# A decoder layer on one core: where the second MLP product's tiles are folded, and when its operands are made

## The chip, the cores and the metric

The kernel runs on one core of a Trainium2 chip. The metric is the device time of one execution in microseconds (us); of several executions the median is given. The engines named below are PE (TensorE, matrix products, with its weight loads as PEld), DVE (VectorE), ACT (ScalarE), POOL (GpSimd) and SP (SyncE, which issues loads). Each works through its own queue in order; an instruction that waits holds up all that stand behind it on its engine.

## The reference, cut to what matters

One layer with 512 tokens and a model width of 1024, in float32:

```python
x = x + mix                                                   # two token mixers, gated
h2 = rmsnorm(x, ln2[i])
x = x + jnp.square(jax.nn.relu(h2 @ w_mlp1[i])) @ w_mlp2[i]   # 1024 -> 4096 -> 1024
h3 = rmsnorm(x, ln3[i])
x = x + jax.nn.sigmoid(h3 @ w_pg[i]) * (p[i] @ w_pp[i])
return rmsnorm(x, ln_f)
```

The change lies in the product with `w_mlp2` and in what follows it: the residual sum, the squares for the norm with `ln3`, and the transposes that the product with `w_pg` needs.

## The kernel before

**Products in three terms.** Each float32 operand is split into a high half that PE takes as it is and a low half, the rest. A product is then three: high by high, low by high, high by low. ACT makes the high half (`hi`, line 319 for weights, 461 for activations), DVE the low one (line 297 for both, shown as `lo` for weights and `ur` for activations).

**The second MLP product in pieces.** The 4096 hidden columns are four chunks. Chunk 0 is done plainly, in two products (`m2_plain`, one for each half of the output columns, four weight units each). Chunks 1 to 3 are done with seven products each in place of eight (Strassen's method, in Winograd's form): A11, S1, S2, S4, A12, S3 and A22 name the weights, and B11, T1, T2, B22, B21, T3 and T4 the hidden operands that go with them. These 21 products stand in the list `MLP2`, which fixes their order; chunks add up in the same PSUM banks, so a bank is complete when its product of chunk 3 is done. A product has two weight units of 128 x 1024, here called half products, with 12 matmuls each, in groups of three. The order of the 21 is A11.1, S1.1, S2.1, A11.2, S1.2, S4.1, S2.2, A11.3, S1.3, S4.2, S2.3, A12.1, S4.3, A12.2, S3.1, S3.2, S3.3, A12.3, A22.1, A22.2, A22.3, with the chunk behind the dot.

**Weights ahead of use.** `weight` calls `fetch`, which at the start of a half product issues the low half for the one two places on (DVE), the high half for the one three on (ACT), the sum that makes S2 or the last S4 four on (DVE, lines 263 and 266), and the loads five on; the first load of S1 and S3 is issued sooner still (SP, line 242), with a second load on POOL's queue that adds to it in place (line 250; line 314 for S4). There are 5 buffers for high halves, 4 for low ones and 8 for raw weights, so a low half cannot be written before PE has left the half product four places back.

**Side work.** Whatever else is to be done is put between the matmuls by `step`, called after each group of three in the 21 products and each eight matmuls in the plain ones. It runs the first entry of the list `later`, and it takes a generator in `side` one stage further each time that `pace` columns (4608 here, nine matmuls of 512) have gone by:

```python
def step(columns=None):
    if later:
        later.pop(0)()
    since[0] += columns or together[0] * pace[0]
```

`hid_operands` is such a generator: for each of the 21 products in their order it makes the sum (two DVE instructions, line 1418 or 609; T products only), then the two high halves (ACT), then the two low ones (DVE). Before the change it is put into `side` between the two plain products.

**The fold.** A token tile of the residual is `x2[m, t, n]`: column half m, token half t, tile n. `onto` (line 1455, DVE) adds a bank or a tile times the norm's factor to it. In Winograd's form the seven products make shared sums: p (A11), u = p + a (bank a is S2's) and w = u + c (bank c is S1's). Tile (0,0) gets p and bank b (A12), (0,1) gets w and bank d (S4), (1,1) gets w and bank x (S3), and (1,0) gets u and bank x after A22 has been added to it. `final` folds the last bank of a tile, squares the tile for the norm (ACT, line 1481), transposes it (PE, line 1486, four transposes, called a turn here) and splits the transposed tile. In the kernel before, p is copied and folded behind A11 of chunk 3; all of u and w is made and folded behind S2 of chunk 3 (`a_done`, `c_done`, `w_done`, lines 1508, 1512 and 1455), which this document calls the joint; and each `final` stands directly behind the last product of its bank.

**Inputs of the end.** The rows of p and the factor of the last norm are loaded on POOL's queue (lines 1548 and 1552) ahead of the 21 products, and p is split as an entry of `later`.

## Time and profile before

| what | value |
|---|---|
| time, median of 3 runs (lowest to highest) | 957.88 us (956.86 to 957.93) |
| profiled execution: its own time | 956.95 us |
| profiled execution: span | 955.1 us |
| instructions | 15091 |
| mean granted clock of PE | 0.995 |
| second MLP product in the span | 726 to 891 us |
| moved by DMA | 150.34 MB, mean 157 GB/s |

The page's second part cuts the span into 40 slices of 23.9 us; the second MLP product is in the 31st to the 38th:

```profile
PE   9999999999999999999999999999999999989997
DVE  7698879866789589878856797677766698997454
PEclk9999999999999999999999999999999999999998
DMA  9474482973818456456562437556557556796202
```

Each digit is a busy share in tenths, 9 being 90% or more. A busy PE is a PE that has a matmul in flight; the granted clock says how fast it may go. A wait is put down to what released it last.

### The profile page before, as it was taken

How to read it: one execution, taken by the hardware profiler on the slowest of the kernel's cores; microseconds unless marked ns; L12 is line 12 of the kernel's file. 1: busy time of each engine (PE TensorE's matmuls, PEld its weight loads, DVE VectorE, ACT ScalarE, POOL GpSimd, SP SyncE). 2: the span in 40 equal slices, each digit the busy share in tenths (PEclk: the TensorE clock that was granted, in tenths of full speed). 3: DMA queues.
4: the chain of work that ended last, by engine and by line, in shares of the span. 5: the costliest groups of instructions: out<-in, count | busy, mean ns of one | idle time of the engine just before them, and what ended most of it. 6: DMA issues, size and time to landing. Idle time of an engine off the chain costs nothing.

```text
span 955.1 us, 15091 instructions
## 1 busy us (share of the span) xinstructions
PE 944.7 (99%) x5892; PEld 851.2 (89%) x5892; DVE 726.7 (76%) x1029; ACT 541.0 (57%) x880; POOL 103.2 (11%) x143
## 2 busy tenths in 40 slices
PE   9999999999999999999999999999999999989997
PEld 8789998899988888999988899999998888868886
DVE  7698879866789589878856797677766698997454
ACT  7357546445675579675723447555655356556543
POOL 0150010120100013021020000011000110010000
PEclk9999999999999999999999999999999999999998
DMA  9474482973818456456562437556557556796202
GB/s 349 141 229 118 128 199 68 293 231 95 199 45 232 157 152 176 123 133 199 157 219 88 128 71 197 135 133 155 156 150 186 149 117 147 217 268 199 67 0 89
DMA packets 46022, 150.34 MB, mean 157 GB/s; under 512 B 6723, under 2 KB 7311, under 8 KB 45952
## 3 DMA queue, kind: packets, MB, share of 16 engines
q1 hardware_dynamic: 29664, 100.61, 30.7%
q0 software_dynamic: 12608, 44.26, 23.5%
q10 hardware_dynamic: 3680, 4.51, 1.3%
q8 instruction: 46, 0.75, 0.3%
q14 instruction: 24, 0.20, 0.1%
HBM read 143.03 MB, written 8.17 MB: 158 GB/s over the span
## 4 chain that ended last, share of the span: by engine, by line
PE 96%; DVE 3%; issue 1%; ACT 0%; POOL 0%; POOLq 0%; DVEq 0%
PE mmt L333 76%; PE smt L333 9%; PE mmt L581 2%; PE smt L1015 1%; DVE lo L297 1%; PE smt L955 1%; PE smt L878 1%; PE smt L553 0%; DVE u L1455 0%; DVE ur L297 0%; PE smt L848 0%; PE smt L972 0%; PE smt L971 0%; PE smt L961 0%; PE smt L847 0%
## 5 line engine op out<-in xcount | busy, mean ns | idle before, releaser
L333 PE MATMUL mmt<-ur,hi 128*128 128x256 f32 (+1 forms) x2320 | 476.0, 302 | 0.0
L333 PEld LDWEIGHTS mmt<-ur,hi 128*128 128x128 f32 x2320 | 373.4, 188 | 16.7
L333 PE MATMUL mmt<-ur,lo 128*128 128x256 f32 (+1 forms) x1160 | 351.2, 303 | 0.0
L297 DVE TENSOR_TENSOR lo<-w,hi 128x1024 fp32r<-128x1024 f32 x248 | 301.3, 1218 | 58.5 <-PE mmt L333 37.4
L319 ACT ACTIVATE hi<-w 128x1024 fp32r<-128x1024 f32 x248 | 259.1, 1054 | 91.5 <-PE mmt L333 21.7
L333 PE MATMUL mmt<-hi,ur 128*128 128x512 f32 (+3 forms) x832 | 240.9, 373 | 0.0
L333 PEld LDWEIGHTS mmt<-ur,lo 128*128 128x128 f32 x1160 | 218.6, 188 | 8.1
L333 PEld LDWEIGHTS mmt<-hi,ur 128*128 128x128 f32 x832 | 150.5, 188 | 25.8
L333 PE MATMUL mmt<-lo,ur 128*128 128x512 f32 (+3 forms) x416 | 154.9, 372 | 0.0
L461 ACT ACTIVATE ur<-u 128x512 fp32r<-128x512 f32 x111 | 66.3, 625 | 88.7 <-DVE u L1279 30.9
L333 PEld LDWEIGHTS mmt<-lo,ur 128*128 128x128 f32 x416 | 78.2, 188 | 13.9 <-DVE lo L297 0.3
L297 DVE TENSOR_TENSOR ur<-u,ur 128x512 fp32r<-128x512 f32 x110 | 72.4, 684 | 12.2 <-ACT ur L461 9.9
L333 PE MATMUL smt<-hi,ur 128*128 128x512 f32 x256 | 80.4, 396 | 0.0
L454 DVE TENSOR_TENSOR u<-u,mmt 128x512 f32<-128x512 f32 (+1 forms) x88 | 54.1, 646 | 26.8 <-PE mmt L333 26.5
L401 ACT ACTIVATE u<-mmt 128x512 f32<-128x512 f32 x72 | 43.0, 598 | 52.7 <-PE mmt L333 52.5
L250 POOL DMA_DIRECT2D w<-in_wts_dram x42 | 40.0, 1005 | 232.5 <-DVE lo L297 72.9
L333 PEld LDWEIGHTS smt<-hi,ur 128*128 128x128 f32 x256 | 48.4, 191 | 9.8
L333 PE MATMUL smt<-lo,ur 128*128 128x512 f32 x128 | 50.6, 395 | 2.0 <-DVE lo L297 2.0
L276 POOL DMA_DIRECT2D w<-in_wts_dram x18 | 16.1, 897 | 316.4 <-DVE w L273 153.5
L333 PEld LDWEIGHTS smt<-lo,ur 128*128 128x128 f32 x128 | 24.4, 191 | 7.6 <-DVE lo L297 2.4
L1389 ACT ACTIVATE u<-u 128x512 f32<-128x512 f32 x24 | 15.0, 628 | 26.7 <-DVE u L1385 26.7
L1250 ACT ACTIVATE u<-u 128x256 f32<-128x256 f32 x32 | 11.4, 409 | 20.8 <-DVE u L454 20.7
(235 smaller groups left out, 838.9 us busy)
## 6 DMA issues: line engine op xcount, KB each, us to landing
w<-in_wts_dram SPq DMA_DIRECT2D x180, 512.0 KB, 4.6
w<-in_wts_dram POOLq DMA_DIRECT2D x64, 512.0 KB, 7.3
u<-in_xT_dram SPq DMA_DIRECT2D x8, 256.0 KB, 5.3
u<-in_ws_dram SPq DMA_DIRECT2D x8, 256.0 KB, 5.4
v_dram<-u ACTq DMA_DIRECT2D x8, 256.0 KB, 6.3
u<-v_dram POOLq DMA_DIRECT2D x8, 256.0 KB, 6.4
y_dram<-u ACTq DMA_DIRECT2D x8, 256.0 KB, 2.0
u<-y_dram POOLq DMA_DIRECT2D x8, 256.0 KB, 6.3
```

The costliest lines, as they stand in the source:

```text
L250: GP.dma_start(w, wts[UNIT[b]], accum_op=OP.add)
L276: GP.dma_start(w, wts[UNIT[f"{q}.A21"]], accum_op=OP.add)
L297: V.tensor_tensor(lo, x, hi.bitcast(F32), op=OP.subtract)
L319: S.activation(hi[:, s], w[:, s], AF.Copy, scale=1.0 if c is None else c)
L333: TE.matmul(o, lhsT=l, rhs=r, start=a, stop=b, skip_group_check=shared)
L401: S.activation(sums[c], bank[b], AF.Copy, scale=-scale if c[0] else scale)
L454: V.tensor_tensor(out, s, ps, op=OP.subtract if m else OP.add)
L461: S.activation(hi, x, AF.Copy)
L581: TE.matmul(q0ps[i], lhsT=(hi, hi, lo)[j][:, c], rhs=(xh, xl, xh)[j], start=not k and not j, stop=k == KC - 1 and j == 2)
L878: TE.matmul(pss[b // 2][:, a * 256 + lo:a * 256 + 256], lhsT=q0[h][:, b * P:(b + 1) * P], rhs=k0[h][:, (b - 1) * P + lo:(b + 1) * P], star ...
L1250: S.activation(outs[n], s[:, halves(n)], AF.Sigmoid)
L1389: S.activation(s, s, AF.Square)
```

## The change

The number and the kind of the sums and folds stay; their places and the tiles that hold them change.

- Behind A11 of chunk 3, p is only copied (ACT), into a tile s of its own. Behind S2 of chunk 3, u and w are only made, each in tiles of its own.
- w is folded onto (0,1) behind A12 of chunk 2 and onto (1,1) behind S3 of chunk 2. s and u are folded onto (0,0) and (1,0) behind A12 of chunk 3.
- `final` of (0,1) stands behind S3 of chunk 1 rather than behind S4 of chunk 3. The others stay behind the product that they stood behind.
- `hid_operands` is put into `side` as soon as the plain operands are split, two weight units before the end of the first plain product.
- The loads of p and of the last norm's factor go behind S3 of chunk 3, and p's split behind A22 of chunk 2.

```diff
@@ m2_plain
             if len(hs) < 8:
                 hid_splits(2)
+                if len(hs) == 8:
+                    side.append(hid_operands())
...
+    def last_inputs():
+        for k in range(2):
+            t = u32()
+            GP.dma_start(t, pT[k * P:(k + 1) * P, :])
+            pt.append(t)
+        for g in range(2):
+            t = u32()
+            GP.dma_start(t, lnf[:, g * 512:(g + 1) * 512].to_broadcast([P, 512]))
+            lnb.append(t)
...
         def p_done(n):
-            u.append(u32())
-            S.activation(u[n], bank["p"][n], AF.Copy)
-            onto(0, 0, n, bank["p"][n])
+            s.append(u32())
+            S.activation(s[n], bank["p"][n], AF.Copy)
 
         def a_done(n):
-            V.tensor_tensor(u[n], u[n], bank["a"][n], op=OP.add)
-            onto(1, 0, n, u[n])
+            u.append(u32())
+            V.tensor_tensor(u[n], s[n], bank["a"][n], op=OP.add)
 
         def c_done(n):
-            V.tensor_tensor(u[n], u[n], bank["c"][n], op=OP.add)
-
-        def w_done(n):
-            for m in range(2):
-                onto(m, 1, n, u[n])
+            w.append(u32())
+            V.tensor_tensor(w[n], u[n], bank["c"][n], op=OP.add)
+
+        def onto_w(m):
+            return lambda n: onto(m, 1, n, w[n])
+
+        def onto_u(n):
+            onto(1, 0, n, u[n])
+
+        def onto_s(n):
+            onto(0, 0, n, s[n])
+
+        last = SEVEN[-1]
+        after = {("A11", last): [p_done], ("S2", last): [a_done, c_done], ("A12", 2): [onto_w(0)], ("S3", 1): [(0, 1, "d", smt)],
+                 ("S3", 2): [onto_w(1)], ("S3", last): [(1, 1, "x", mmt)], ("A12", last): [onto_s, (0, 0, "b", smt), onto_u],
+                 ("A22", last): [(1, 0, "x", smt)]}
...
-            for f in {"A11": (p_done,), "S2": (a_done, c_done, w_done)}.get(op, ()):
-                later.extend(lambda f=f, n=n: f(n) for n in range(2))
-            if op in ("S4", "S3", "A12", "A22"):
-                (m, t), turns = {"S4": ((0, 1), smt), "S3": ((1, 1), mmt), "A12": ((0, 0), smt), "A22": ((1, 0), smt)}[op]
+            for f in after.get((op, c), ()):
                 for n in range(2):
-                    final(m, t, n, bank[b][n], turns)
+                    if callable(f):
+                        later.append(lambda f=f, n=n: f(n))
+                    else:
+                        final(*f[:2], n, bank[f[2]][n], f[3])
+            if (op, c) == ("S3", last):
+                last_inputs()
+            elif (op, c) == ("A22", 2):
+                later.append(lambda: pt.__setitem__(slice(0, 2), [split(t) for t in pt]))
...
     m2_plain(0)
-    side.append(hid_operands())
     m2_plain(1)
-    for k in range(2):
-        t = u32()
-        GP.dma_start(t, pT[k * P:(k + 1) * P, :])
-        pt.append(t)
-    for g in range(2):
-        t = u32()
-        GP.dma_start(t, lnf[:, g * 512:(g + 1) * 512].to_broadcast([P, 512]))
-        lnb.append(t)
-    later.append(lambda: pt.__setitem__(slice(0, 2), [split(t) for t in pt]))
     m2_seven()
```

## The prediction, as it was made before the changed kernel ran

> **What bounds the kernel now.** I read the busy shares first, then the stretches of 10 us in the stage that is changed, then the waits of PE, then the chain and the timeline around the one wait that is left.

> ```profile
> PE 944.7 (99%) x5892; PEld 851.2 (89%) x5892; DVE 726.7 (76%) x1029; ACT 541.0 (57%) x880; POOL 103.2 (11%) x143
> ```

> PE is the bound over the whole span, so only time in which PE stands still or runs slowly can be won. The stretches (columns: stretch, length, busy us of PE, PEld, DVE, ACT, POOL, then granted clock, DMA share, GB/s):

> ```profile
> 830.00:840.00 10.00, 10.00 (x45) 8.02 (x44) 9.93 (x15) 5.92 (x9) 2.07 (x3) 1.00 0.97 277
> 840.00:850.00 10.00, 7.54 (x30) 5.51 (x29) 10.00 (x13) 2.44 (x6) 1.45 (x2) 0.83 1.03 245
> 870.00:880.00 10.00, 10.00 (x53) 8.27 (x51) 6.28 (x7) 6.38 (x11) 0.00 (x0) 1.00 0.61 168
> 880.00:890.00 10.00, 10.00 (x48) 8.31 (x47) 4.96 (x5) 3.95 (x5) 0.00 (x0) 1.00 0.60 188
> ```

> In 840 to 850 PE has 2.46 us idle, the granted clock is 0.83, and DVE has no gap at all. PE's waits from 720 us to the end are two:

> ```profile
> PE smt L333 <- DVE lo L297: 2.0, 1, 2.0
> PE smt L1486 <- DVE u L1455: 0.5, 1, 0.5
> ```

> The first is a product of A12 of chunk 2 that waits for the low half of its weights (L297); the second is a transpose (L1486) of a final tile that waits for its fold (L1455). In microseconds of 1 the granted clock (third figure from the right) is seen low right behind the first wait, which ends at 842.94:

> ```profile
> 843.00:844.00 1.00, 1.00 (x3) 0.80 (x4) 1.00 (x2) 0.00 (x0) 0.00 (x0) 0.57 1.00 193
> 844.00:845.00 1.00, 1.00 (x4) 0.80 (x3) 1.00 (x3) 0.00 (x0) 0.79 (x1) 0.50 1.01 201
> 845.00:846.00 1.00, 1.00 (x4) 0.72 (x3) 1.00 (x3) 0.00 (x0) 0.09 (x1) 0.50 1.09 213
> 846.00:847.00 1.00, 1.00 (x5) 0.81 (x4) 1.00 (x2) 0.00 (x0) 0.00 (x0) 0.72 1.05 225
> ```

> The clock that is missing adds up to 0.43 + 0.50 + 0.50 + 0.28 = 1.71 us of PE work not done. So the wait costs its own 1.95 us and 1.7 us more.

> Why the low half is late is read from DVE's timeline (start, length, line, what); the steps below are differences of these starts:

> ```profile
> 824.63 1.22 DVE L297 TENSOR_TENSOR lo<-w,hi 128x1024 fp32r<-128x1024 f32 x1
> 825.77 1.21 DVE L266 TENSOR_TENSOR w<-w 128x1024 f32<-128x1024 f32 x1
> 826.90 1.21 DVE L297 TENSOR_TENSOR lo<-w,hi 128x1024 fp32r<-128x1024 f32 x1
> 828.04 1.22 DVE L266 TENSOR_TENSOR w<-w 128x1024 f32<-128x1024 f32 x1
> 829.17 1.28 DVE L297 TENSOR_TENSOR ur<-u,ur 128x512 fp32r<-128x512 f32 x2
> 830.38 1.22 DVE L297 TENSOR_TENSOR lo<-w,hi 128x1024 fp32r<-128x1024 f32 x1
> 831.51 0.68 DVE L1508 TENSOR_TENSOR u<-u,mmt 128x512 f32<-128x512 f32 x1
> 832.22 0.75 DVE L1455 SCALAR_TENSOR_TENSOR u<-u,nrm 128x512 f32<-128x512 f32 x1
> 832.89 1.29 DVE L1418 TENSOR_TENSOR u<-u 128x512 f32<-128x512 f32 x2
> 834.10 0.68 DVE L1508 TENSOR_TENSOR u<-u,mmt 128x512 f32<-128x512 f32 x1
> 834.81 0.75 DVE L1455 SCALAR_TENSOR_TENSOR u<-u,nrm 128x512 f32<-128x512 f32 x1
> 835.48 1.28 DVE L1512 TENSOR_TENSOR u<-u,smt 128x512 f32<-128x512 f32 x2
> 836.68 1.22 DVE L297 TENSOR_TENSOR lo<-w,hi 128x1024 fp32r<-128x1024 f32 x1
> 837.81 0.74 DVE L1455 SCALAR_TENSOR_TENSOR u<-u,rtok 128x512 f32<-128x512 f32 x1
> ...
> 840.47 1.28 DVE L297 TENSOR_TENSOR ur<-u,ur 128x512 fp32r<-128x512 f32 x2
> 841.67 2.35 DVE L297 TENSOR_TENSOR lo<-w,hi 128x1024 fp32r<-128x1024 f32 x2
> ```

> No row has an idle time behind it: DVE is a full queue. A product has two half products, each with its own weights, of which DVE makes a low half of 1.14 us (824.63 to 825.77). The low half at 830.38 and the one two places on, at 841.67, lie 11.29 us apart, while PE uses up two half products in 5.44 us (below). What fills the queue between them are the joint's four sums (L1508, L1512) and six folds (L1455).

> **What the loss is in all.** PE's timeline, the first row of the seven-product part, two around the wait, the first behind the part; then from the chain a run of matmuls and a turn:

> ```profile
> 769.41 0.39 PE L333 MATMUL smt<-hi,ur 128*128 128x512 f32 x1
> 840.37 0.61 PE L333 MATMUL smt<-hi,ur 128*128 128x512 f32 x2
> 842.94 0.64 PE L333 MATMUL smt<-lo,ur 128*128 128x512 f32 x1 [1.95 <-DVE lo L297]
> 891.26 0.39 PE L333 MATMUL mmt<-hi,ur 128*128 128x512 f32 x1
> 785.89 10.88 PE smt L333 x48
> 849.63 0.44 PE smt L1486 x4
> ```

> Three matmuls take 10.88 / 16 = 0.680 us, so a half product (12) takes 2.72 and a product 5.44. I number the half products of the 21 products from 0 to 41. They are 168 groups of three, 114.24 us; six turns (four transposes of a finished tile each) lie among them, 6 x 0.44 = 2.64. From 769.41 PE could begin the next product at 769.41 + 114.24 + 2.64 = 886.29; it does at 891.26. The stage loses 4.97 us: 0.23 by 840.37 (769.41 + 70.72 = 840.13 was due), 1.95 in the wait, 1.71 in the clock, 0.50 at the transpose, and 0.58 in small pieces around them.

> **The change part by part.** DVE does the same number of sums and folds as before; they are only put elsewhere.

> (a) The joint. Today 4 sums and 6 folds stand behind S2 of chunk 3, and 2 folds behind A11. After it there are 4 sums alone, and behind A11 only ACT's two copies. The folds go behind A12 of chunk 2, S3 of chunk 2, and A12 of chunk 3. Ahead of the low half for A12 (chunk 2) this takes out two folds of 0.67 (832.22 to 832.89, 834.81 to 835.48) and four in 837.81 to 840.47, 2.66: 4.00 us. The two behind A11 come on top, 1.3 us, unless DVE idles there.
> When is that low half late? Half 26 begins at 769.41 + 26 x 2.72 = 840.13 and needs it as its third matmul, 0.45 later, at 840.58. DVE ends it near 842.9. If DVE stood at 824.63 exactly where it stands now, 4.00 us less put it at 838.9, a margin of 1.7; the low half before it (836.68 today) moves 1.34 up and ends at 836.5 against 837.86. That is the worst case for DVE.

> (b) The operands' sums and splits begin at the third quarter of the first plain product in place of the second plain product. By the pace this moves each such pair of DVE steps (1.20 us, 829.17 to 830.38) some two products up; the density in mid-stage stays the same, because a pair is only replaced by a later one. The 3.6 us that come first fall into 737 to 748, where DVE idles:

> ```profile
> 742.47 1.22 DVE L297 TENSOR_TENSOR lo<-w,hi 128x1024 fp32r<-128x1024 f32 x1 [4.21 <-PE smt L333]
> 807.75 1.22 DVE L297 TENSOR_TENSOR lo<-w,hi 128x1024 fp32r<-128x1024 f32 x1 [1.55 <-PE mmt L333]
> ```

> So (b) costs nothing there. It pays at the end: all operands are split by the start of S3, and the folds moved there meet a DVE without them. At 807.75 DVE waits for a buffer that PE still reads: there it is as far ahead as it can be, before and after, and I count on from that low half's end, 808.89. Up to the low half of half 25 come, today, 8 low halves and 4 weight sums (L263, L266) at 1.14, 7 pairs at 1.20, 4 sums at 0.60 and 4 folds at 0.67, 27.2 us: 836.1, where the trace has 837.8, so 1.7 us of small waits. The new order has the same without the folds, 24.5: 833.4, with the small waits 835.1. The next low half (one pair between, 2.34) ends at 835.7 to 837.4 against 840.58, the one after it at 838.1 to 839.8 against 843.3. I take the later ends; neither these nor the worst case of (a) gives a wait.

> (c) The final tile of S4 is folded after S3 of chunk 1, in half 30, its transposes in half 31 at 769.41 + 31 x 2.72 + 0.68 = 854.4. Its two folds then stand behind the low half for S3 of chunk 3, which cannot start before PE leaves half 28 (848.3): they end near 851. The 0.50 us wait goes. The PSUM pair that S4 holds longer is next wanted by the transposes of (1,1), at about 870: free.

> (d) Folds in S3, A12 and A22: in a half product DVE has at most a low half, two folds and two splits or folds more, 1.14 + 4 x 0.65 = 3.7 us, and the half beside it 2.5 at most: 6.2 against PE's 5.44, taken from a lead of 3 us or more. The rows of 870 to 890 show 3.7 and 5.0 us of DVE free in 10. Cost 0.

> (e) The loads of p and of the last norm go from POOL's queue before the stage to behind S3, their split (2 on ACT, 2 on DVE) to the last half pair.

> ```profile
> 844.21 0.88 POOL L250 DMA_DIRECT2D w<-in_wts_dram  x1 [3.64 <-DVE lo L297]
> DMA to landing us min/median/max: 5.7/8.6/10.5
> u<-in_pT_dram POOLq DMA_DIRECT2D x2, 256.0 KB, 3.4
> ```

> The accumulating load at 844.21 (landing times of the six from 818 on in the second row, of p's in the third) is the last on POOL's queue before them, and nothing but the small norm step stands behind. Issued when PE ends S3, 769.41 + 34 x 2.72 + 0.88 = 862.8, or sooner, they land by 874 even at 10.5 us; the split is due when half 40 begins (769.41 + 40 x 2.72 + 2.64 = 880.9), its use at 886. ACT and DVE have room there (last stretch). 1 MB more in 862 to 875 meets a DMA share of 0.6 to 0.8. Cost 0; its other end, p landing 5 us later than the longest seen, would leave 2 us of wait.

> Sum: 4.97 off. From the profiled execution's own 956.95 (span 955.1 and 1.85 around it) that is 951.98; from the median of the runs shown, 957.88, it is 952.91. Two runs in four, the profiled one counted, lie near each, so I predict **952.4**.

> [...]

> **The rivals.**
> 1. The clock's fall has another cause or does not come in each execution: 4.97 - 1.71 = 3.26 off, 954.1 (off 957.4, the middle of the two). For it: nothing but that 0.83 is seen in one execution; against it: the fall begins as the wait ends. [...] 0.07.
> 2. A wait is left: PE meets one late operand or a transpose a little early, half a microsecond, and the clock still falls: 0.5 + 1.7 kept, 954.6. For it: ACT and DVE wait on each other in order, and high halves of weights stand behind operand splits on ACT. 0.10.
> 3. The change doesn't do what it says: DVE's total is the same, and it was full for 20 us (9.93 and 10.00 of 10 in the first rows); the wait only moves to S3, where the folds now are: 957.4 less 0 to 1.5, within 0.2%. Against it: (d). 0.07.
> 4. Slower: S3 becomes bound by its accumulating loads. Each half of S3 needs two loads of 512 KB, and the DMA share is 0.97 to 1.03 in 830 to 850. One wait of ACT's high half for a load is there already:

> ```profile
> 836.70 1.06 ACT L319 ACTIVATE hi<-w 128x1024 fp32r<-128x1024 f32 x1 [0.90 <-DMA w<-in_wts_dram]
> ```

> The last accumulating load, issued at 844.21, lands by 854.7 at the longest; PE, 5 us earlier, needs that low half (half 33) at 769.41 + 33 x 2.72 + 0.88 + 0.45 = 860.5, and thus, a high half of 1.06 and a low one of 1.22 ahead, the landing by 858.2. It decides from a landing later than 858.2, 3.5 us over the longest seen; slower by 0.2% needs a landing at 863.4 (a wait of 5.2 and the clock's 1.7 make 4.97 + 1.9): some 960. Against it: loads are issued when DVE frees their buffer, and DVE is earlier. 0.04.

> **How the numbers follow.** Forecast 0.72 (951 to 953.8), rivals 0.07, 0.10, 0.07, 0.04. 0.2% (1.9 us) is about what a measurement of this kernel tells from no change: faster means under 956.0. Faster: 0.72 + 0.07 + 0.09 = 0.88; same 0.08; slower 0.04. The range takes in the forecast and rivals 1 and 2: 951.0 to 955.6.

> **What would show it.** Right: no wait of PE on L297 or on a fold between 830 and 892; granted clock 1.00 in 840 to 850; the product after the stage begins near 886.3; DVE's folds spread over 845 to 880. Wrong: a wait of PE in S3 or on the p operand near 886, ACT's hi halves waiting for a DMA in 845 to 860, or a clock under 1 with no wait ahead of it.

## The result, and the profile after

| | kernel before | kernel after |
|---|---|---|
| median (lowest to highest), 4 runs each | 957.72 us (956.86 to 957.93) | 951.88 us (951.71 to 952.52) |
| ratio of the two, 95% interval | | 0.9942 (0.9925 to 0.9959) |
| profiled execution, its own time | 956.95 us | 951.71 us |
| its span | 955.1 us | 949.6 us |
| mean granted clock of PE in it | 0.995 | 0.998 |

The kernel became 0.58% faster. The forecast was 952.4 with a range of 951.0 to 955.6. The busy times of the page after stand against those of before; DVE's is the same to 0.2 us, so it does the same work:

```profile
PE 941.3 (99%) x5892; PEld 849.4 (89%) x5892; DVE 726.5 (77%) x1029; ACT 540.8 (57%) x880; POOL 102.9 (11%) x143
```

The same stretches of 10 us, after the change (columns as before):

```profile
830.00:840.00 10.00, 10.00 (x46) 8.29 (x45) 10.00 (x14) 6.54 (x9) 2.62 (x3) 1.00 1.01 264
840.00:850.00 10.00, 10.00 (x46) 8.29 (x45) 9.45 (x13) 3.89 (x5) 3.06 (x5) 1.00 1.05 308
870.00:880.00 10.00, 10.00 (x50) 8.30 (x49) 8.31 (x10) 6.13 (x11) 0.00 (x0) 1.00 0.52 157
880.00:890.00 10.00, 10.00 (x46) 8.29 (x45) 5.30 (x8) 4.20 (x9) 0.00 (x0) 1.00 0.35 105
```

In 840 to 850 PE has 10.00 us busy where it had 7.54, at a clock of 1.00 where it had 0.83. The view of PE's waits from 720 to 955 us has no row left. DVE is still nearly full in 830 to 850 (10.00 and 9.45 us of 10); what changed is what it does there. Its timeline at the joint, after:

```profile
827.15 1.23 DVE L297 TENSOR_TENSOR lo<-w,hi 128x1024 fp32r<-128x1024 f32 x1
828.29 0.69 DVE L1520 TENSOR_TENSOR u<-u,mmt 128x512 f32<-128x512 f32 x1
828.88 1.30 DVE L609 SCALAR_TENSOR_TENSOR u<-u 128x512 f32<-128x512 f32 x2
830.09 0.69 DVE L1520 TENSOR_TENSOR u<-u,mmt 128x512 f32<-128x512 f32 x1
830.69 1.29 DVE L1524 TENSOR_TENSOR u<-u,smt 128x512 f32<-128x512 f32 x2
831.88 1.23 DVE L297 TENSOR_TENSOR lo<-w,hi 128x1024 fp32r<-128x1024 f32 x1
833.02 1.30 DVE L297 TENSOR_TENSOR ur<-u,ur 128x512 fp32r<-128x512 f32 x2
834.22 1.23 DVE L297 TENSOR_TENSOR lo<-w,hi 128x1024 fp32r<-128x1024 f32 x1
...
849.00 1.41 DVE L1455 SCALAR_TENSOR_TENSOR u<-mmt,rtok,u 128x512 f32<-128x512 f32 x2
```

Between the low half at 827.15 and the one at 834.22, two places on, lie 7.07 us, where there were 11.29: the four sums (L1520, L1524) are there, the six folds are not. The last row is the final fold of (0,1), at its new place.

How long the stage takes is read from PE's timeline, its first row and the first row behind it:

```profile
768.72 0.62 PE L333 MATMUL smt<-hi,ur 128*128 128x512 f32 x2
885.75 0.39 PE L333 MATMUL mmt<-hi,ur 128*128 128x512 f32 x1
```

885.75 - 768.72 = 117.03 us, where it took 121.85 (769.41 to 891.26). With nothing lost it would be 116.88 (114.24 of products, 2.64 of turns). So 4.82 of the 4.97 us were won.

**Where the rest of the 5.24 us comes from.** The two profiled executions differ by 5.24 us. 0.69 of it lies ahead of the stage, which begins at 768.72 rather than 769.41. It comes from the kernel's first microseconds, where no code differs. PE's timeline from 0 to 20 us, second row, before:

```profile
5.04 15.22 PE L581 MATMUL mmt<-ur 128*128 128x512 f32 x62
```

And after:

```profile
5.18 15.07 PE L581 MATMUL mmt<-ur 128*128 128x512 f32 x65 [0.33 <-ACT ur L566]
```

By 20.25 us PE has done three more matmuls of this line, and three at the 0.227 us apart that a 0.680 us group shows are 0.68. In the trace's records of the clock the first stretch at full clock begins at 6.87 us in the execution before and at 4.34 in the one after. Behind the stage the execution after is 0.27 us longer (951.71 - 885.75 = 65.96; 956.95 - 891.26 = 65.69). 0.69 + 4.82 - 0.27 = 5.24.

### The profile page after: what moved, and what is told of

Its sections match the earlier page's. It is cut to its first block, busy times and chain, and to the rows that moved or that the text cites. A ratio compares the mean times of both kernels' runs of the same rounds, so it can differ in the third digit from the quotient of the medians.

```text
span 949.6 us, 15089 instructions
## 1 busy us (share of the span) xinstructions
PE 941.3 (99%) x5892; PEld 849.4 (89%) x5892; DVE 726.5 (77%) x1029; ACT 540.8 (57%) x880; POOL 102.9 (11%) x143
## 4 chain that ended last, share of the span: by engine, by line
PE 98%; issue 1%; DMA 0%; ACT 0%; DVE 0%; POOLq 0%; POOL 0%; DVEq 0%
PE mmt L333 78%; PE smt L333 10%; PE mmt L581 2%; PE smt L1015 2%; PE smt L955 1%; PE smt L878 1%; PE smt L848 0%; PE smt L972 0%; PE smt L961 0%; PE smt L847 0%; PE smt L971 0%; PE smt L1310 0%; PE smt L1171 0%; PE smt L1071 0%; DMA cv<-in_vec_dram 0%
## 5 line engine op out<-in xcount | busy, mean ns | idle before, releaser
L333 PE MATMUL mmt<-ur,hi 128*128 128x256 f32 (+1 forms) x2320 | 476.0, 302 | 0.0
L333 PEld LDWEIGHTS mmt<-ur,hi 128*128 128x128 f32 x2320 | 373.1, 188 | 16.6
L333 PE MATMUL mmt<-ur,lo 128*128 128x256 f32 (+1 forms) x1160 | 351.2, 303 | 0.0
L297 DVE TENSOR_TENSOR lo<-w,hi 128x1024 fp32r<-128x1024 f32 x248 | 302.1, 1221 | 56.9 <-PE mmt L333 35.9
L319 ACT ACTIVATE hi<-w 128x1024 fp32r<-128x1024 f32 x248 | 259.2, 1054 | 93.8 <-PE mmt L333 24.5
L333 PE MATMUL mmt<-hi,ur 128*128 128x512 f32 (+3 forms) x832 | 241.1, 374 | 0.0
L333 PEld LDWEIGHTS mmt<-ur,lo 128*128 128x128 f32 x1160 | 218.6, 188 | 8.2
L333 PEld LDWEIGHTS mmt<-hi,ur 128*128 128x128 f32 x832 | 150.3, 188 | 25.7
L333 PE MATMUL mmt<-lo,ur 128*128 128x512 f32 (+3 forms) x416 | 154.8, 372 | 0.0
L333 PEld LDWEIGHTS mmt<-lo,ur 128*128 128x128 f32 x416 | 78.2, 188 | 13.6
L297 DVE TENSOR_TENSOR ur<-u,ur 128x512 fp32r<-128x512 f32 x110 | 72.7, 688 | 11.8 <-ACT ur L461 9.5
L333 PE MATMUL smt<-hi,ur 128*128 128x512 f32 x256 | 79.1, 390 | 0.0
L250 POOL DMA_DIRECT2D w<-in_wts_dram x42 | 40.2, 1001 | 246.1 <-DMA w<-in_wts_dram 94.0
L333 PEld LDWEIGHTS smt<-hi,ur 128*128 128x128 f32 x256 | 47.8, 188 | 9.8
L333 PE MATMUL smt<-lo,ur 128*128 128x512 f32 x128 | 49.8, 389 | 0.0
L333 PEld LDWEIGHTS smt<-lo,ur 128*128 128x128 f32 x128 | 24.0, 188 | 5.0
(235 smaller groups left out, 838.1 us busy)
## 6 DMA issues: line engine op xcount, KB each, us to landing
u<-in_xT_dram SPq DMA_DIRECT2D x8, 256.0 KB, 5.3
u<-in_ws_dram SPq DMA_DIRECT2D x8, 256.0 KB, 5.4
v_dram<-u ACTq DMA_DIRECT2D x8, 256.0 KB, 6.6
u<-v_dram POOLq DMA_DIRECT2D x8, 256.0 KB, 6.2
y_dram<-u ACTq DMA_DIRECT2D x8, 256.0 KB, 2.0
u<-y_dram POOLq DMA_DIRECT2D x8, 256.0 KB, 6.2
```

The lines of the kernel that those rows point to most:

```text
L250: GP.dma_start(w, wts[UNIT[b]], accum_op=OP.add)
L297: V.tensor_tensor(lo, x, hi.bitcast(F32), op=OP.subtract)
L319: S.activation(hi[:, s], w[:, s], AF.Copy, scale=1.0 if c is None else c)
L333: TE.matmul(o, lhsT=l, rhs=r, start=a, stop=b, skip_group_check=shared)
```

## The experiments

Letters are those of the prediction's steps: (a) the folds leave the joint, (b) operands early, (c) the final tile of S4 later, (d) folds in S3 and later, (e) the last inputs later. The theory is that the loss comes from DVE's full queue at the joint alone, and that (a) takes it away. The rivals: (b) is what gains, as DVE's lead; the place of (c) is needed; the clock's fall is not caused by the wait. Ratios are against the kernel before, measured beside each group: a median of 957.81 us in 19 runs for e1, e2, e3 and the ten sums, 957.68 in 13 for e4 and the seven to nine sums, 957.75 in 10 for e5.

### The folds alone: e1_folds_only

The kernel after, with the operands' generator and the last inputs at their old places. All folds and finals stand as after the change, so (c) and (d) are in it beside (a).

```diff
-                if len(hs) == 8:
-                    side.append(hid_operands())
...
-            if (op, c) == ("S3", last):
-                last_inputs()
-            elif (op, c) == ("A22", 2):
-                later.append(lambda: pt.__setitem__(slice(0, 2), [split(t) for t in pt]))
...
+    side.append(hid_operands())
     m2_plain(1)
+    last_inputs()
+    later.append(lambda: pt.__setitem__(slice(0, 2), [split(t) for t in pt]))
```

> The folds and finals stand as in the changed kernel; the operands' sums and splits begin between the two plain products and the loads and the split of p stand ahead of the 21 products, as before the change. Theory (the six folds at the joint alone made the low half of half 26 late): 4.0 us are out of DVE's queue ahead of it, which leaves a margin of 1.7 us, so PE has no wait in the stage, the granted clock stays 1.00, the stage from its first matmul to the next product takes 117.0 to 117.3 us, and the time is that of the changed kernel, 951.7 to 952.5. Rival (the early operands are what gives DVE its lead): a wait of 1 to 2 us on L297 stays near 840, with the lower clock behind it, and the time is 955 to 957.7.

Measured: 951.89 us (951.37 to 952.9, 4 runs), ratio 0.9938 (0.9923 to 0.9953). No wait of PE in the stage, the stage 117.02 us. DVE's timeline of this kernel, the low halves of halves 25 and 26:

```profile
832.74 1.23 DVE L297 TENSOR_TENSOR lo<-w,hi 128x1024 fp32r<-128x1024 f32 x1
833.87 1.30 DVE L297 TENSOR_TENSOR ur<-u,ur 128x512 fp32r<-128x512 f32 x2
835.08 2.37 DVE L297 TENSOR_TENSOR lo<-w,hi 128x1024 fp32r<-128x1024 f32 x2
```

The low half of half 26 ends at 835.08 + 1.14 = 836.2. It is due at 768.72 + 26 x 2.72 + 0.45 = 839.9: a margin of 3.7 us without any help from (b). The folds and finals at their new places give the whole gain, without (b) and (e).

### Operands and inputs alone: e2_early_only

The kernel before, with (b) and (e); joint and finals unchanged.

```diff
             if len(hs) < 8:
                 hid_splits(2)
+                if len(hs) == 8:
+                    side.append(hid_operands())
...
+            if (op, c) == ("S3", SEVEN[-1]):
+                last_inputs()
+            elif (op, c) == ("A22", 2):
+                later.append(lambda: pt.__setitem__(slice(0, 2), [split(t) for t in pt]))
...
-    side.append(hid_operands())
...
```

> The operands begin early and p's loads and split stand late, as in the changed kernel; the joint and all folds are as before the change. Theory: the six folds are still in DVE's queue; from the changed kernel's queue and the folds added back, the low half of half 26 ends 0.8 to 1.9 us after PE wants it, so the wait on L297 stays with the lower clock behind it, the gain over the kernel before is 0 to 1.5 us, and the time is 956 to 957.7. Rival (the early operands do it): no wait, 951.7 to 952.5.

Measured: 955.73 us (955.19 to 956.83, 10 runs), ratio 0.9978 (0.9969 to 0.9988): about 2 us gained, a little more than expected. Whether (b) or (e) gains them was not taken apart. PE's timeline of this kernel, its two waits:

```profile
841.23 0.50 PE L333 MATMUL smt<-lo,ur 128*128 128x512 f32 x1 [1.33 <-DVE lo L297]
...
846.57 0.66 PE L1488 MATMUL smt<-ident,u 128*128 128x128 f32 x4 [2.10 <-DVE u L1455]
```

The wait for the low half is 1.33 in place of 1.95. The clock did not fall in the profiled execution (1.00 from 820 to 860 us), and yet the 1.71 us of it were not won: the wait of the transposes is 2.10 in place of 0.50. The fold that they wait for stands in DVE's full queue, whether PE before it runs fully or at half clock. Eight of the ten executions have a mean clock of 0.997 or 0.998 (955.19 to 956.12), two have 0.995 (956.79 and 956.83).

### The final tile of S4 at its old place: e3_final_back

The kernel after, with the fold of w onto (0,1) and the final of (0,1) behind S4 of chunk 3.

```diff
-        after = {("A11", last): [p_done], ("S2", last): [a_done, c_done], ("A12", 2): [onto_w(0)], ("S3", 1): [(0, 1, "d", smt)],
+        after = {("A11", last): [p_done], ("S2", last): [a_done, c_done], ("S4", last): [onto_w(0), (0, 1, "d", smt)],
```

> The changed kernel, with the fold of w onto (0,1) and the final of (0,1) put back directly behind S4 of chunk 3. Theory (the 0.5 us wait at the transposes came from the full queue, not from the place): DVE has a lead of over 4 us there, folds the tile 1 us or more ahead of its transposes, and the time is the changed kernel's within 0.3 us: 951.7 to 952.3, no wait of PE. Rival (the place itself is too early): a wait of about 0.5 us on L1455 near 842, 952.4, or 954 if the clock falls behind it.

Measured: 951.87 us (951.41 to 952.6, 4 runs), ratio 0.9937 (0.9922 to 0.9952), no wait of PE. With the joint unburdened the old place costs nothing; the wait at the transposes came from the queue ahead of the fold, not from the place. (b) and (e) are in this kernel, too; the old place without them was not run.

### The inputs at their old place: e4_inputs_early

The kernel after with `last_inputs()` and p's split ahead of the 21 products, as in the first diff, (b) kept.

> The changed kernel with the loads of p and of the last norm's factor, and p's split, put back ahead of the 21 products. These hold six tiles of the 67 through the stage, besides the up to 64 in use by my count. Theory (the place of the inputs costs and gives nothing by itself): new tiles may wait for PE to leave old ones, which takes away some of DVE's lead near the eighth product, but the lead of over 4 us bears it: no wait of PE, 951.5 to 952.5. Rival (the tiles are what the inputs' new place pays for): a wait of PE of over 0.5 us between 800 and 850, 952.5 to 955.

Measured: 951.87 us (951.61 to 951.97, 4 runs), ratio 0.994 (0.9926 to 0.9955), no wait of PE; the stage is 117.03 us again (769.30 to 886.33). DVE's waits from 760 to 850 have a row that the kernel after does not have:

```profile
DVE ur L297 <- PE mmt L333: 5.4, 4, 1.8
```

DVE's splits of operands wait for tiles that PE still reads. The low half of half 25 begins at 834.82 rather than 831.88, some 3 us later, or 2.4 when the later start of this stage (0.58) is taken off. It ends at 835.96 and is due at 769.30 + 25 x 2.72 + 0.45 = 837.75, a margin of 1.8 us where the kernel after has 4.2. So with (b) the place of the inputs is worth lead, and here no time. That the six tiles which the inputs hold are the reason fits the wait, but was not tried by itself.

### Doubling the suspect: seven, eight, nine and ten sums put back at the joint

In the kernel after, k sums of a tile that nobody reads stand on DVE behind the joint's sums, ahead of the low half of half 25. With this the length of PE's wait can be chosen.

```diff
         def c_done(n):
             w.append(u32())
             V.tensor_tensor(w[n], u[n], bank["c"][n], op=OP.add)
+            if n:
+                t = u32()
+                for _ in range(k):
+                    V.tensor_tensor(t, w[0], w[1], op=OP.add)
```

> The changed kernel with ten more DVE sums of 128x512, 0.60 us each, that nothing reads, behind the sums of w at the joint: 6.0 us more in DVE's queue, ahead of the low half of half 25, which has a lead of 4.15 us (it ends at 833.02 and is wanted at 837.17). So PE waits 1.9 us there. Theory (such a wait brings half clock behind it): granted clock near 0.83 in the ten us that follow, 1.7 us more lost: 3.4 to 4.0 over the changed kernel, 955.3 to 955.9. Rival (the lower clock of the kernel before has another cause, or comes in some executions only): the wait alone, 953.6 to 954. [...]

> The changed kernel with seven more DVE sums behind the sums of w, which nothing reads. Ten of them took 7.15 us (0.715 each, since they write one tile) and left PE waiting 3.1 us; seven take 5.0, so PE waits about 0.95 us for the low half of half 25. Theory (the clock falls when PE stands idle for more than some 55 to 60% of one of the 3.41 us stretches in which the granted clock is seen to change): 0.95 is 28% at most, the clock stays at 1.00, 952.7 to 953.0. Rival (any wait of PE for a product's weights brings the clock down): 954.4 to 954.7.

> As with seven, but eight such sums: a wait of about 1.65 us, 48% of a stretch at most. Theory: no lower clock, 953.4 to 953.7, in nearly all executions. Rival: 955.1 to 955.5.

> As with seven, but nine such sums: a wait of about 2.4 us, 70% of a stretch if it lies in one. Theory: the clock falls in about half of the executions, where the wait lies in one stretch, and not where it is cut in two: 954.1 to 954.4 without, 955.8 to 956.1 with. Rival: 955.8 to 956.1 in all of them.

| sums | median (lowest to highest), runs | ratio, 95% interval | wait of PE in the profiled execution | above the kernel after |
|---|---|---|---|---|
| 7 | 952.65 (952.49 to 953.01), 4 | 0.9949 (0.9935 to 0.9964) | 0.91 | 0.77 |
| 8 | 953.38 (953.16 to 953.62), 4 | 0.9957 (0.9941 to 0.9974) | 1.64 | 1.50 |
| 9 | 954.82 (954.13 to 958.41), 10 | 0.9975 (0.9965 to 0.9984) | 2.37 | 2.94 |
| 10 | 957.21 (956.67 to 957.62), 10 | 0.9996 (0.9986 to 1.0006) | 3.10 | 5.33 |

PE's timeline with eight sums:

```profile
838.83 0.50 PE L333 MATMUL mmt<-lo,ur 128*128 128x512 f32 x1 [1.64 <-DVE lo L297]
```

With ten sums, the wait and the stretch behind it:

```profile
840.28 0.68 PE L333 MATMUL mmt<-lo,ur 128*128 128x512 f32 x1 [3.10 <-DVE lo L297]
```

```profile
840.00:850.00 10.00, 9.72 (x36) 7.88 (x37) 10.00 (x14) 5.25 (x8) 3.06 (x5) 0.83 0.83 200
```

With seven and eight the time rises by about the wait and by nothing else, at a mean clock of 0.997 or more in all executions. With ten it rises by the wait (3.1), by 1.7 of clock (0.17 of 10 us) and by 0.5 that I did not place. With nine it is mixed: six executions at 954.13 to 954.83 with 0.997 or 0.998, three at 955.29 to 955.90 with 0.996, one at 958.41 with 0.996. So the clock's fall does hang on PE's wait, but not every wait brings it. The kernel with ten sums came out 1.3 us over what was expected because the sums took 0.72 us each rather than 0.60.

### The kernel before, looked at again: b_look1, b_look2, b_look3

No edit.

> The kernel before, once more, for the profile of another execution. Theory: DVE alone sets when the transposes of (0,1) may run, by its fold near 848, whatever PE's clock does between. If the wait on L297 (1.95 us) lies mostly in one of the 3.41 us stretches, the clock falls behind it and the wait at the transposes is 0.5; if it is cut in two, the clock stays at 1.00 there, the wait at the transposes is 0.5 + 1.7 = 2.2, and the clock may fall behind this one, 1 us longer in all (957.7 to 958.4); with neither, 956.2 to 956.6. Rival: the lower clock always follows the first wait, and the times differ for another reason.

> As the first look at the kernel before: one of the three cases, told by the time and by where the granted clock is low.

> As the first look at the kernel before: one of the three cases, told by the time and by where the granted clock is low.

Times: 956.93, 957.66 and 957.72 us. PE's timeline in the first:

```profile
842.92 0.50 PE L333 MATMUL smt<-lo,ur 128*128 128x512 f32 x1 [1.98 <-DVE lo L297]
848.27 0.66 PE L1486 MATMUL smt<-ident,u 128*128 128x128 f32 x4 [0.61 <-DVE u L1455]
```

In the second:

```profile
842.05 0.50 PE L333 MATMUL smt<-lo,ur 128*128 128x512 f32 x1 [1.96 <-DVE lo L297]
...
847.39 0.66 PE L1486 MATMUL smt<-ident,u 128*128 128x128 f32 x4 [2.10 <-DVE u L1455]
```

And the microseconds of the second (granted clock third from the right):

```profile
845.00:846.00 1.00, 0.29 (x2) 0.00 (x0) 1.00 (x2) 0.00 (x0) 0.00 (x0) 1.00 1.03 229
...
847.00:848.00 1.00, 0.61 (x5) 0.61 (x6) 1.00 (x3) 0.63 (x2) 0.00 (x0) 0.98 1.04 246
848.00:849.00 1.00, 1.00 (x4) 0.70 (x3) 1.00 (x1) 1.00 (x5) 0.00 (x0) 0.50 1.04 270
...
851.00:852.00 1.00, 1.00 (x5) 0.77 (x4) 1.00 (x2) 1.00 (x3) 0.00 (x0) 0.81 0.99 389
```

The first look is like the execution that the prediction was made from: the clock falls behind the first wait (0.67 in 844 to 845, 0.50 in 845 to 847), and the second wait is short, 0.61. In the second look the clock stays full behind the first wait (1.00 from 842 to 847), the second wait is 2.10, and the clock falls behind that one (0.50 from 848 to 851). Its stage takes 891.98 - 768.51 = 123.47 us, 6.59 lost where 4.97 were. The third look is like the second (waits 1.98 and 2.08, 123.45 us). So the kernel before has at least two ways through the stage, 1.6 us apart. Of its 32 executions in the first two groups of runs (19 and 13), 11 lie at 956.82 to 957.10 with a mean clock of 0.995, 19 at 957.67 to 958.98, and two at 956.25 and 956.54 with 0.998. The ten of the third group are less clear: six at 957.72 to 958.09, three at 957.04 to 957.20, and one at 956.03 with a mean clock of 0.996. Of these kinds only the first two have a trace; that the clock did not fall at all in the two at 0.998 is read from that figure alone.

### Only the final tile of S4 moved: e5_final_late

The kernel before with the final of (0,1) behind S3 of chunk 1; the joint as it was.

```diff
+            if (op, c) == ("S3", 1):
+                for n in range(2):
+                    final(0, 1, n, bank["d"][n], smt)
...
-            if op in ("S4", "S3", "A12", "A22"):
+            if op in ("S3", "A12", "A22"):
...
```

> The kernel before, with the final of (0,1) alone moved behind S3 of chunk 1, as in the changed kernel; the six folds stay at the joint, operands and inputs stay as before. The wait on L297 stays at about 2 us, that at the transposes is gone, so DVE no longer sets when PE goes on. Theory: the lower clock behind the first wait now costs its 1.7 us where it comes, and nothing covers it: executions with it (mean clock 0.995 or 0.996) at 956.2 to 956.8, those without (0.997 or 0.998) at 954.5 to 955.2. Rival (the fold and the clock are independent, and the transposes' wait is 0.5 us and no more): all at 956.2 to 957.2.

Measured: 955.33 us (954.12 to 956.33, 7 runs), ratio 0.9976 (0.9965 to 0.9988). PE's only wait in the stage, from its timeline:

```profile
843.00 0.69 PE L333 MATMUL smt<-lo,ur 128*128 128x512 f32 x1 [1.98 <-DVE lo L297]
```

The microseconds behind it:

```profile
844.00:845.00 1.00, 1.00 (x4) 0.81 (x3) 1.00 (x3) 0.00 (x0) 0.00 (x0) 0.50 1.02 201
...
846.00:847.00 1.00, 1.00 (x5) 0.77 (x4) 1.00 (x2) 1.00 (x2) 0.00 (x0) 0.72 1.05 242
```

The first wait is as before, the transposes wait no more. Three executions lie at 956.15 to 956.33 with a mean clock of 0.995, four at 954.12 to 955.33 with 0.997. Here, where no second wait follows, the clock's fall shows in the time; in the kernel before the second wait swallows it (0.50 and 0.61 behind a fall, 2.10 and 2.08 without one).

No kernel was clearly faster than the changed one (e1, e3 and e4 have its time within 0.01 us by the median), and none could be much faster by this means: PE has no wait in the stage, and 98% of its chain is PE.

## Why the prediction was right, by its own steps

- **The bound and the cause.** Right. DVE's queue at the joint was the cause: with the folds and finals moved and nothing else the whole gain is there (e1); with the final of (0,1) alone moved the first wait stays at 1.98 (e5); with its place undone nothing is lost (e3); and sums put back bring PE's wait back, about us for us in the time (seven and eight sums).
- **(a)** Right, and its margin was underrated. 1.7 us was the worst case for half 26; the folds and finals by themselves leave 3.7 (e1), since the two folds behind A11 and the lead before them count as well.
- **(b)** Cost 0, right. The low halves of 25 and 26 end at 833.0 and 835.4 against the later ends of 835.1 and 837.4 that I took; due at 837.2 and 839.9, they have 4.2 and 4.5 us. But (b) is not needed for the gain (e1). Together with (e) it pays where the joint is full (e2, about 2 us).
- **(c)** The time of the folds was right: they begin at 849.00 and end at 850.4 ("near 851"), the turns at 853.89 by the chain. That the move takes the 0.50 wait away is only half right: with the joint unburdened it goes at the old place too (e3).
- **(d)** Cost 0, right: no wait of PE from S3 on.
- **(e)** Cost 0, right, but "or sooner" was 20 us sooner. ACT's and POOL's rows in the timeline of the kernel after:

```profile
842.76 1.47 POOL L1501 DMA_DIRECT2D u<-in_pT_dram  x2
...
846.09 1.06 ACT L319 ACTIVATE hi<-w 128x1024 fp32r<-128x1024 f32 x1 [2.81 <-DMA w<-in_wts_dram]
...
851.30 1.06 ACT L319 ACTIVATE hi<-w 128x1024 fp32r<-128x1024 f32 x1 [4.14 <-DMA w<-in_wts_dram]
```

p's loads are issued at 842.76, when nothing on POOL's queue holds them, and land 10.2 us later (median) rather than 3.4, beside the loads of S3. This is what I had named as a sign against me, high halves that wait for a DMA in 845 to 860, and it came: 2.81 and 4.14 us. It costs nothing. The second of them is that of half 33. It ends at 852.4, the low half at 853.6, and PE needs it at 768.72 + 33 x 2.72 + 0.88 + 0.45 = 859.8: 6.2 us to spare. The waits for loads that rival 4 named came, and were too short to reach PE. The other end that (e) gives, 2 us of wait for a p that lands 5 us later than the longest seen, does not come out of its own numbers: 862.8 + 15.5 = 878.3 is still ahead of 880.9, when the split is due.

- **The sum.** 4.97 predicted for the stage, 4.82 measured. Two of its terms were booked wrongly, though: 1.71 for the clock and 0.50 for the transposes are not independent. In the chain of the profiled execution before, DVE carries the end:

```profile
842.88 1.14 DVE lo L297
844.02 1.20 DVE ur L297 x2
...
846.35 1.21 DVE lo L297
847.56 0.68 DVE u L1455
848.24 0.04 issue
848.28 0.66 PE smt L1486 x4
```

PE goes on at 848.28 because DVE's fold ends then, however it spent the time from 842.9. At half clock it lost 1.71 and waited 0.50, together 2.21; at full clock it would have waited about 2.1 (2.10 and 2.08 in the later looks and 2.10 in e2). The sum comes out because it was taken as a whole, as the distance of 891.26 from 886.29, and the change removes the whole queue; the split into terms had no part in it.

- **Rival 1** was priced wrongly for that reason: had the clock not fallen, not 1.71 but about 0.1 us less would have been there to win. Its mechanism (the fall does not hang on the wait) is out: in the stage no fall comes without a wait (the kernel after, e1, e3, e4), none behind 0.91 or 1.64 us, and one behind 1.95 to 1.98 (the kernel before, e5) and 3.10 (ten sums); the 2.37 us with nine sums bring none in the one execution that has a trace. That it does not come behind the same wait in each execution is true: in b_look2 it comes behind the wait of 2.10 and not behind that of 1.96.
- **Rival 2** (a wait of half a microsecond and the clock's 1.7): no wait was left, and the price was wrong: the wait of 0.91 brought no fall.
- **Rival 3** is out: DVE is nearly as full as before in 830 to 850, and PE waits nowhere, since the work there is no longer ahead of a due operand.
- **The level.** I took the middle of 951.98 (from the profiled execution) and 952.91 (from the median). The measured 951.88 is near the first, and by more than one term: from 951.98 the start gave 0.69 less, stage and tail 0.15 and 0.27 more, which makes 951.71 for the profiled one. The 0.69 is not the change's doing, so that the two lie within 0.1 us is in part luck. The second fails at "957.88 less 4.97": the median execution of before is of the kind of b_look2, which loses 6.59 in the stage, and the change wins that as well.

## What to carry to other kernels

When one wait of PE is left, look at everything that stands in the releasing engine's queue ahead of the awaited instruction, and ask which of it is due later: here six folds cost some 5 us by their place. Terms of a loss on one chain do not add up when a later wait on the same engine follows; take away the first in thought and see how much longer the second gets. And look at several executions of a kernel before booking a clock's fall: the median may be of another kind than the profiled one.

## What the runs showed of the hardware

| run | wait of PE | share of 3.413 us | end of the wait | half clock behind it |
|---|---|---|---|---|
| seven sums | 0.91 | 27% | 838.13 | none up to 850 |
| e2, first wait | 1.33 | 39% | 841.23 | none up to 860 |
| eight sums | 1.64 | 48% | 838.83 | none up to 850 |
| kernel before | 1.95 | 57% | 842.94 | from 843.14 |
| b_look2, first wait | 1.96 | 57% | 842.05 | none up to the second wait |
| b_look3, first wait | 1.98 | 58% | 842.09 | none up to the second wait |
| b_look1 | 1.98 | 58% | 842.92 | from 844.34 |
| e5_final_late | 1.98 | 58% | 843.00 | from 843.16 |
| b_look3, second wait | 2.08 | 61% | 847.43 | from 848.00 |
| b_look2, second wait | 2.10 | 62% | 847.39 | from 847.96 |
| e2, second wait | 2.10 | 62% | 846.57 | none up to 860 |
| nine sums | 2.37 | 69% | 840.07 | none up to 850 |
| ten sums | 3.10 | 91% | 840.28 | 0.83 in 840 to 850 |

No fall comes behind the waits up to 1.64 us, and one behind that of 3.10. From 1.95 to 2.37 both are seen, so there the length of the wait alone does not tell. An estimate of mine for the looks counts back from the start of each fall by 3.413 us. In the kernel before, b_look1 and e5 the wait in front of the fall then lies within one stretch (in the kernel before from 839.72 to 843.14, the wait from 840.99 to 842.94; in b_look1 by 0.01 us only), and so do the second waits of b_look2 and b_look3. The first wait of b_look2 (840.09 to 842.05) is cut near 841.13 into 1.04 and 0.92, that of b_look3 near 841.17, and neither brings a fall. For e2 and nine sums no fall is seen to count from, and whether their waits were cut is not shown; nor is whether the spread of the executions with nine sums comes from this, as only one of them has a trace. The 55 to 60% in the expectation for seven sums is likewise an estimate, near the 57% of the kernel before; a border as such was not shown.

At the end of the kernel, where PE's last matmuls are of 128 columns, the clock falls behind less idle time. Two stretches of 1 us of the kernel before:

```profile
948.00:949.00 1.00, 0.13 (x2) 0.00 (x0) 0.40 (x2) 0.83 (x3) 0.00 (x0) 0.97 0.12 43
949.00:950.00 1.00, 0.00 (x0) 0.00 (x0) 0.52 (x3) 0.44 (x3) 0.06 (x1) 0.50 0.00 0
```

PE stands still from 948.13 and the clock falls at 948.95, so 0.82 us of the 3.413 ahead of the fall were idle, 24%. In the kernel after PE stands still from 942.64 and the clock falls at 946.42, 3.78 us later. So idle time is not all that counts. What else does was not tried.

**Sums on one tile.** The ten sums that write one and the same tile take 7.23 us, 0.72 each, where the joint's two sums of L1524, of the same size, begin 0.60 apart (1.19 from 830.69 to 831.88 for both, in the kernel after). DVE's timeline of the kernel with ten sums:

```profile
831.86 7.23 DVE L1528 TENSOR_TENSOR u<-u 128x512 f32<-128x512 f32 x10
```

The expectation for seven sums gives the common target as the reason. Sums into ten different tiles were not tried, so that is an estimate; what the runs show beside it are sums whose tile the next instruction reads. In the kernel before a fold that reads the tile of the sum just ahead of it begins as late (0.71, from 831.51 to 832.22), and in e2 too (0.72, from 829.79 to 830.51). In the kernel after, the same sum (L1520), followed by an instruction that does not touch its tile, is followed 0.59 later (828.29 to 828.88).
